# One decoder layer for a prompt and eight samples: the samples' attention in a written PE order, weights fetched by ScalarE, the first half's output projection and norm inside it

## Chip, cores and metric

The kernel runs on one core of a Trainium2 chip. The metric is the device time of one execution in microseconds, as the median of several runs. The engines are TensorE (PE in the profile, PEld for its weight loads), VectorE (DVE), ScalarE (ACT), GpSimd (POOL) and SyncE (SP, which here only issues DMAs).

## What is computed

One layer of a hybrid decoder on a prompt of 512 tokens and on 8 samples of 8 tokens with a cache of 4096 positions each: 576 token columns with the same weights. Cut to what matters here:

```python
h = x * (1 + ada[1]) + ada[0]
z = h @ w_in                       # latents, rotary key, short convolution, gates g_a and g_c
o = attention(...)                 # prompt: causal; samples: over 32 cached pages of 128 rows
y_a = o @ w_oa
y_c = (b_g * conv_y) @ w_oc
m = sigmoid(g_a) * y_a + sigmoid(g_c) * y_c
x = layer_norm(ALPHA * x + g1 * (m @ w_o), ln1_g, ln1_b)
h2 = x * (1 + sc2) + sh2
f = (silu(h2 @ w_ff1) * (h2 @ w_ff3)) @ w_ff2
y = layer_norm(ALPHA * x + g2 * f, ln2_g, ln2_b)
```

The samples' attention works in latent space, with an online softmax: for each page the scores of a sample's 64 query rows (8 heads x 8 tokens) against the page's 256 latent values and 32 rotary values per position, a running maximum and sum, and the weighted sum of the latents.

## The kernel before

Activations lie with features on the partitions and tokens in the columns. The 576 columns are two halves of 288 (`HT`): the first half is all prompt, the second is 224 columns of the prompt and the 64 of the samples. Every dense product is exact in fp32 from three matmuls (`mm3`, L117 to L119): the weight is split into a high and a low part (`wh` on ScalarE, L57; `wl` on VectorE, L60), the activations likewise. A weight comes in chunks of [128, 512] fp32, 256 KB, into a ring `wr` of three, and its split goes into rings `wh` and `wl` of three (`wload`, L99). A weight tile of 1024 columns and one half of the tokens take 24 matmuls of 288 columns.

The stages in order: conditioning and modulated input; latent projections; the prompt's attention (`prompt_units`, L496), among which the convolution's products and the rest of the conditioning are spread; the samples' attention (`sample_units`, L606), among which the gates' products, `w_oc` and the first half of `w_oa` are spread (`fill_gates`, `fill_oa`); then `w_o` and the first norm for the first half, `w_oa`, `w_o` and the norm for the second (loop at L916); then the feed forward and the second norm.

The samples' attention runs over 36 units: four pairs of samples, and for each pair one unit of the step's own 8 rows and eight units of 4 pages for each of the two samples. A page unit does, on PE: four score matmuls of 512 columns (L630, tile `sc`), where the two samples of the pair use different column halves of the array, two rotary score matmuls (L632), four transposes of the weights (L653), eight value matmuls (L661, tile `pv`), two samples again on two column halves. Between them VectorE takes the maximum (L646), ScalarE the exponential, and ScalarE copies the transposed weights to `pT`. A unit's pages are eight DMAs of 256 KB (L569) into a ring of seven tiles `raw`, and four gathers of rotary rows by GpSimd (L573) into a ring of three tiles `kr`.

What sets the order: a scheduler places each engine's instructions by what it expects to be ready, except on engines named in `tc.manual_schedule`, which keep the order of the code. In the samples' stage that is SP alone, so the pages' DMAs and the weights' DMAs stand in SP's queue as the code writes them, and PE's order is the scheduler's. `merge` (L745) spreads the filling units, each a whole product of 48 matmuls, over the attention's units.

In the prompt's attention two heads share the array's column halves in the value matmuls (L543); both heads' transposes (L536) and copies come before, head 0 first.

`Norm` (L812) adds the residual row by row. With `j0 == 8`, the first half's case, it subtracts the mean of all rows at once (`center`) and sums squares; else it takes the mean of the first rows off early.

## Time and profile before

| | |
|---|---|
| time, median of 3 runs (lowest, highest) | 1171.45 us (1170.65, 1172.48) |
| profiled execution, first to last instruction (span) | 1174.0 us |
| mean granted PE clock in it | 0.974 |
| PE busy | 1091.8 us, 93% |
| VectorE / ScalarE / GpSimd busy | 46% / 37% / 19% |
| moved by DMA | 190.07 MB, mean 162 GB/s |

The profile is of one execution; its times are those of the profiled execution, 2.55 us longer than the median. Records of matmuls overlap, since PE is pipelined, so a busy PE isn't a PE at its peak: how many matmuls end per microsecond says more. An fp32 matmul leaves two records; a matmul of split parts one. "Idle before" is the time for which an engine had nothing to run ahead of an instruction, with what ended it; in the chain of waits each row is a start, a length and what ran or was waited for.

### The profile page before, as it was taken

The numbers are of one execution on the slowest core, as the hardware profiler recorded it, in microseconds if no ns is written. First come the engines' busy times: TensorE is split into PE (matmuls) and PEld (weight loads), VectorE is DVE, ScalarE is ACT, GpSimd is POOL, SyncE is SP. The second block draws the span as 40 slices with busy tenths as digits, with TensorE's granted clock in tenths as the row PEclk, the third lists the DMA queues.
The fourth block names the chain that finished last, engine by engine and source line by source line (L and its number), as shares of the span: only waits on it lengthen the run. The fifth ranks groups of instructions, "written<-read, shape, count | busy, mean of one in ns | idle before, by whom it ended". The sixth has DMA issues, their size and how long they took to land.

```text
span 1174.0 us, 19868 instructions
## 1 busy us (share of the span) xinstructions
PE 1091.8 (93%) x7646; PEld 931.6 (79%) x7646; DVE 537.7 (46%) x1059; ACT 431.7 (37%) x859; POOL 225.1 (19%) x232
## 2 busy tenths in 40 slices
PE   6889999998798899989999889899999999999994
PEld 5878787785466466556569889899999999999994
DVE  3476354443132333332247787933233333355656
ACT  2474343435232522332346355332223222334433
POOL 1120000023442342441301421800000000001303
PEclk9999999999799998999999899999999999999998
DMA  9626354418389586696675423032222222455551
GB/s 366 209 96 204 122 185 141 140 46 311 106 294 321 170 300 214 220 310 244 203 239 172 159 73 108 3 107 91 90 72 79 100 75 72 118 178 150 157 181 54
DMA packets 84941, 190.07 MB, mean 162 GB/s; under 512 B 11600, under 2 KB 15568, under 8 KB 84848
## 3 DMA queue, kind: packets, MB, share of 16 engines
q1 hardware_dynamic: 80752, 180.42, 45.8%
q0 software_dynamic: 4096, 8.40, 2.3%
q8 instruction: 60, 0.98, 0.3%
q14 instruction: 33, 0.27, 0.1%
HBM read 185.72 MB, written 3.06 MB: 161 GB/s over the span
## 4 chain that ended last, share of the span: by engine, by line
PE 48%; DVE 7%; DMA 5%; issue 2%; ACT 1%; SPq 1%; POOL 0%; POOLq 0%; ACTq 0%; DVEq 0%
PE acc L117 10%; PE acc L118 9%; PE acc L119 9%; PE sc L117 4%; PE sc L119 4%; PE sc L118 4%; PE sc L630 3%; DMA wr<-in_w_ff_dram 3%; PE pv L661 3%; DVE xr L60 2%; DVE wl L60 2%; ACT wh L57 1%; PE sc L632 1%; SPq L569 1%; DMA raw<-in_page_dram 1%
## 5 line engine op out<-in xcount | busy, mean ns | idle before, releaser
L117 PE MATMUL acc<-h,wl 128*128 128x288 f32 x960 | 288.7, 302 | 14.1 <-DVE wl L60 8.5
L118 PE MATMUL acc<-h,wh 128*128 128x288 f32 x960 | 286.9, 299 | 2.0 <-DVE h L60 1.5
L119 PE MATMUL acc<-h,wh 128*128 128x288 f32 x960 | 284.7, 297 | 1.9 <-issue 1.9
L60 DVE TENSOR_TENSOR wl<-wr,wh 128x512 fp32r<-128x512 f32 (+1 forms) x186 | 178.7, 966 | 212.1 <-ACT wh L57 206.1
L57 ACT ACTIVATE wh<-wr 128x512 fp32r<-128x512 f32 (+2 forms) x196 | 156.6, 807 | 194.5 <-DMA wr<-in_w_ff_dram 58.7
L117 PEld LDWEIGHTS acc<-h,wl 128*128 128x128 f32 x960 | 181.5, 189 | 25.9 <-DVE wl L60 11.2
L118 PEld LDWEIGHTS acc<-h,wh 128*128 128x128 f32 x960 | 182.2, 190 | 7.3 <-issue 5.0
L119 PEld LDWEIGHTS acc<-h,wh 128*128 128x128 f32 x960 | 182.6, 190 | 3.1 <-issue 2.9
L573 POOL DMA_INDIRECT kr<-in_krT_dram,idx x128 | 122.7, 959 | 227.4 <-ACT krh L57 103.0
L117 PE MATMUL sc<-h,wl 128*128 128x288 f32 x336 | 99.9, 297 | 0.0
L118 PE MATMUL sc<-h,wh 128*128 128x288 f32 x336 | 99.4, 296 | 0.0
L119 PE MATMUL sc<-h,wh 128*128 128x288 f32 x336 | 99.1, 295 | 0.0
L630 PE MATMUL sc<-raw,qa 128*64 128x512 f32 x256 | 85.3, 634 | 3.2 <-DMA raw<-in_page_dram 1.8
L60 POOL TENSOR_TENSOR xr<-xr,h 128x288 f32<-128x288 f32 x16 | 17.2, 1098 | 366.1 <-ACT h L57 362.5
L117 PE MATMUL acc<-f,wl 128*128 128x288 f32 x288 | 85.9, 298 | 1.6 <-DVE wl L60 1.6
L118 PE MATMUL acc<-f,wh 128*128 128x288 f32 x288 | 84.9, 295 | 0.0
L119 PE MATMUL acc<-f,wh 128*128 128x288 f32 x288 | 84.7, 294 | 0.0
L661 PE MATMUL pv<-raw,pT 128*64 128x256 f32 x512 | 68.8, 401 | 12.5 <-ACT pT L57 6.3
L661 PEld LDWEIGHTS pv<-raw,pT 128*64 128x64 f32 x512 | 38.5, 143 | 37.7 <-issue 16.0
L119 PEld LDWEIGHTS sc<-h,wh 128*128 128x128 f32 x336 | 63.6, 189 | 0.0
L118 PEld LDWEIGHTS sc<-h,wh 128*128 128x128 f32 x336 | 63.3, 189 | 0.1
L117 PEld LDWEIGHTS sc<-h,wl 128*128 128x128 f32 x336 | 63.2, 188 | 0.1
(326 smaller groups left out, 1767.1 us busy)
## 6 DMA issues: line engine op xcount, KB each, us to landing
raw<-in_page_dram SPq DMA_DIRECT2D x256, 256.0 KB
wr<-in_w_ff_dram SPq DMA_DIRECT2D x76, 512.0 KB
wa<-in_w_ada_dram SPq DMA_DIRECT2D x40, 512.0 KB
wr<-in_w_in_dram SPq DMA_DIRECT2D x64, 256.0 KB
wr<-in_w_ff_dram SPq DMA_DIRECT2D x16, 384.0 KB
wr<-in_w_o_dram SPq DMA_DIRECT2D x18, 256.0 KB
wr<-in_w_oa_dram SPq DMA_DIRECT2D x16, 256.0 KB
x<-in_xT_dram SPq DMA_DIRECT2D x4, 576.0 KB
```

The costliest lines, as they stand in the source:

```text
L57: nc.scalar.activation(out=out, in_=in_, func=func, **kw)
L60: return (eng or v).tensor_tensor(out=out, in0=in0, in1=in1, op=op)
L117: mm(ps, lhsT=wl, rhs=xh, start=start, stop=False)
L118: mm(ps, lhsT=wh, rhs=xl, start=False, stop=False)
L119: mm(ps, lhsT=wh, rhs=xh, start=False, stop=stop)
L569: dma(out=raw[:, j], in_=a["page"][bass.ds(vs[GP * e + j], 1)].rearrange("a p d -> p (a d)"))
L573: g.indirect_dma_start(kr[:, 128 * j:128 * j + 128], None, a["krT"], bass.IndirectOffsetOnAxis(ap=idx[:, i:i + 1], axis=0))
L630: mm(ps[rows(e), :n], lhsT=qa[:, c, 2 * pa + e], rhs=rhs, start=c == 0, stop=False)
L632: mm(ps[:, :n], lhsT=qr[:, i, pa].rearrange("p e q -> p (e q)"), rhs=kx, start=False, stop=i == 0)
L661: mm(pv[rows(e), :KVL], lhsT=pT[:np_, j, e], rhs=rhs, start=j == 0, stop=j == nj - 1)
```

## The change

Four things are changed together.

1. In the samples' stage PE joins SP in the written order. `sample_units` becomes `sample_stage`: a unit is cut into `rotary` (the rotary rows' split, one unit earlier), `turn` (transposes and copy), `scores` (now with maximum, exponential and the running sum) and `values`. Between them the code calls `fill`: always behind the values, and in about half of the units also between `turn` and the next unit's `scores`.
2. The filling work is cut finer, into 59 pieces: half a gate tile (24 matmuls), one tile of `w_oc`, `w_oa` (12 matmuls) or `w_o`. Its weights are fetched by DMAs on ScalarE's queue.
3. `fill_wo` is new filling work: the first half's `w_o` products, residual, norm and modulated input, with its rows in the gates' tiles. So the loop over both halves behind the stage is now the second half alone. `w_o` is loaded in both places, where before its split was kept for both halves. The first half's rows and norm are copied by DMA to `xr` and `rst1` afterwards.
4. In the prompt's attention head 1's transposes come first.

```diff
-    def wload(src, n=1024, hl=None, tag="", to=None, eng=None):
+    def wload(src, n=1024, hl=None, tag="", to=None, eng=None, q=None):
...
-            dma(out=raw[:, :m], in_=src[:, c:c + m])
+            (q or dma)(out=raw[:, :m], in_=src[:, c:c + m])
...
+    wq = nc.scalar.dma_start
+
+    def dense_chunks(i, dst):
+
+        w = wload(a["w_in"][i - 3], q=wq)
+        pss = [ps_acc(), ps_acc()]
+        for p in range(2):
+            gpart(pss, w[p], hs, 0, range(4 * p, 4 * p + 4), 8)
+            if p:
+                for ps, sl in zip(pss, sls):
+                    act(dst[:, sl], ps[:, :HT])
+            yield 1
...
-                pts = []
-                for o in range(2):
+                pts = {}
+                for o in (1, 0):
...
+        S = scores(*units[0], pages[0], krn)
         for i, u in enumerate(units):
             if len(pages) <= i + AHEAD < len(units):
                 pages.append(load(*units[i + AHEAD]))
...
+            more = i + 1 < len(units)
+            if more:
+                kx = krn if units[i + 1][1] < 0 else rotary(pages[i + 1])
+            pT = turn(*u, S)
+            fill(2 * i)
+            if more:
+                S = scores(*units[i + 1], pages[i + 1], kx)
+            values(*u, pT, pages[i])
+            fill(2 * i + 1)
+            if u[1] < 0 and u[0] or not more:
+                attended(u[0] - 1 if more else u[0])
...
+    def fill_wo():
+
+        xa = gates["gc"][:, :, :HT]
+        wq(out=xa, in_=a["xT"][:, :, :HT])
+        for k in range(0, 8, 2):
+            g.tensor_scalar(out=xa[:, k:k + 2], in0=xa[:, k:k + 2], scalar1=ALPHA, scalar2=None, op0=MULT)
+        ga = gates["ga"]
+        names = ["ssum", "mu", "qs", "rs", "rr", "sq0", "sq1"]
+        p = Scratch(names, [ga[:, j, :HT] for j in range(8)])
+        n = Norm(p, xa, 0, 8)
...
+        for j in range(8):
+            w = wload(a["w_o"][j], q=wq)
+            ps = ps_acc()
+            gemm([ps], w, [halves(M[0])])
+            n.row(j, ps[:, :HT], ada[:, 2])
+            yield 1
+        n.center()
+        yield 1
+        yield 1
...
+        n.finish(rst, modulate(Q(), gs, bs, rst, H2, HT))
+        gates["xa"], gates["rst"] = xa, rst
+        yield 1
...
+    extra = 59 - 2 * PF - len(units)
+
+    def fill(s):
+
+        i = s // 2
+        if s % 2 or (i + 1) * extra // len(units) > i * extra // len(units):
+            next(F, None)
+    with tc.manual_schedule(engines={mybir.EngineType.SP, mybir.EngineType.PE}):
+        sample_stage(A3, qa, qr, pages, fill)
+        for _ in F:
+            pass
...
+    for j in range(8):
+        to_m(j, 1, woa(j, g), LN)
+    dma(out=xr[:, :, :HT], in_=gates["xa"])
+    dma(out=rst1[:, :HT], in_=gates["rst"])
...
+    def product(j):
+        w = wload(a["w_o"][j])
+        ps = ps_acc()
+        gemm([ps], w, [halves(M[1])])
+        return ps[:, :HT]
+    H2 = htile()
+    n = Norm(LN, xr[:, :, HT:], 1, 6)
+    n.rows(product, ada[:, 2])
+    n.sums()
```

What this does to the instructions is best seen in three places. First PE at the end of the prompt's attention, its last pair of heads; before, the rows are these (`sc<-ident,S` are transposes, `pv<-pt,vt` the value matmuls of one head and key block):

```order
L543 MATMUL pv<-pt,vt 64x512
L536 MATMUL sc<-ident,S 128x128 x3
L543 MATMUL pv<-pt,vt 64x512
L536 MATMUL sc<-ident,S 128x128 x2
L543 MATMUL pv<-pt,vt 64x384
L536 MATMUL sc<-ident,S 128x128 x2
L543 MATMUL pv<-pt,vt 64x384
```

Now PE has there:

```order
L553 MATMUL pv<-pt,vt 64x512 x2
L546 MATMUL sc<-ident,S 128x128 x4
L553 MATMUL pv<-pt,vt 64x384 x2
L546 MATMUL sc<-ident,S 128x128 x2
L553 MATMUL pv<-pt,vt 64x256 x2
```

The two heads' matmuls of a key block, which transposes parted, are now neighbours; so they are in all 16 key blocks, and in none before.

Second, the samples' stage. On PE before, in the pages of the second pair (`sc<-raw,qa` are score matmuls against pages, `sc<-krx,qr` the rotary ones, `pv<-raw,pT` the values):

```order
L630 MATMUL sc<-raw,qa 64x512
L653 MATMUL sc<-ident,S 128x128 x2
L630 MATMUL sc<-raw,qa 64x512 x3
L632 MATMUL sc<-krx,qr 128x512 x2
L653 MATMUL sc<-ident,S 128x128 x2
L630 MATMUL sc<-raw,qa 64x512
L661 MATMUL pv<-raw,pT 64x256 x8
L630 MATMUL sc<-raw,qa 64x512 x3
```

PE now, in a unit without the second piece of filling work, at the place where `w_oa` ends and `w_o` begins:

```order
L118 MATMUL acc<-ol,wh 128x288
L119 MATMUL acc<-oh,wh 128x288
L670 MATMUL sc<-ident,S 128x128 x4
L644 MATMUL sc<-raw,qa 64x512 x4
L646 MATMUL sc<-krx,qr 128x512 x2
L683 MATMUL pv<-raw,pT 64x256 x8
L117 MATMUL acc<-h,wl 128x288
```

All 32 page units have this form, with 24 (for `w_oa` 12) weight matmuls behind the values; before, 17 of the 32 had one score matmul apart from the other three. Between the first score matmul of the stage and the last values stand 900 weight matmuls before and 1152 now. ScalarE's queue, which had no DMA in it, reads in a unit of the gates now:

```order
L107 DMA wr<-in_w_in_dram 128x512
L57 ACTIVATE krh<-kr 128x512
L57 ACTIVATE S,sm<-sc,sm 128x512
L57 ACTIVATE sm<-sm 128x1
L57 ACTIVATE gct<-acc 128x288 x2
L57 ACTIVATE wh<-wr 128x512
L57 ACTIVATE pT<-sc 128x512
L107 DMA wr<-in_w_in_dram 128x512
```

A weight's split (`wh<-wr`) stands between the unit's exponential (`S,sm`) and the copy of the transposed weights (`pT`), and the next fetch into the same ring behind it. On GpSimd the four steps that scale the first half's residual (L909) stand behind all 128 gathers.

Third, the end of the stage. PE has there, from the last unit's scores on (`sc<-ga,ones` are the norm's sums, first of the rows and then of the squares, `sc<-ident,acc` transposes the last pair's attended latents, `sc<-raw` starts their product with the value weights):

```order
L644 MATMUL sc<-raw,qa 64x512 x4
L646 MATMUL sc<-krx,qr 128x512 x2
L683 MATMUL pv<-raw,pT 64x256 x8
L822 MATMUL sc<-ga,ones 128x288
L670 MATMUL sc<-ident,S 128x128 x4
L683 MATMUL pv<-raw,pT 64x256 x8
L837 MATMUL sc<-ga,ones 128x288
L699 MATMUL sc<-ident,acc 128x128 x2
L117 MATMUL sc<-raw 128x128
```

ScalarE has there (`ga<-gct` squares rows for the norm, `qs_80` and `raw` take the attended latents, `h` is a modulated row, `oh` the attention's result for the samples):

```order
L57 ACTIVATE ga<-gct 128x288 x8
L57 ACTIVATE qs_80<-sc 128x2x8x8 x2
L154 ACTIVATE ga<-ga 128x288
L57 ACTIVATE raw<-qs_80 128x8x16 x2
L155 ACTIVATE ga<-ga 128x288
L57 ACTIVATE h<-hf_6963,ga 128x288
L57 ACTIVATE h<-hf_6967,ga 128x288
L57 ACTIVATE h<-hf_6971,ga 128x288
L57 ACTIVATE h<-hf_6975,ga 128x288
L57 ACTIVATE oh<-sc 64x4x64
L57 ACTIVATE h<-hf_6979,ga 128x288
L57 ACTIVATE oh<-sc 64x4x64
```

The moved norm's last steps stand among the last steps of the attention; before, the norm's steps all came behind the stage, and the last transposes stood among `w_oa`'s matmuls of the first half.

More of the change, by code (lines that the diff above doesn't have):

```diff
@@ L687, in sample_units @@
         smt, acct = {}, {}
-        nxt = scores(*units[0], pages[0])
+        S = scores(*units[0], pages[0], krn)
         for i, u in enumerate(units):
@@ L745, in merge @@
-    def merge(s, f, nf, ns):
-        done, i = 0, 0
-        while i < ns and next(s, None) is not None:
-            i += 1
-            while done * ns < i * nf:
-                u = next(f, None)
-                if u is None:
-                    break
-                done += u
-    S, F = prompt_units(), fill_ca()
-    merge(S, F, 12, 18)
-    for _ in F:
-        pass
-    close(E2)
-    close(E)
-    close(CV)
-    gates["pool"] = pool("gc", side="right")
-    gates["gc"] = gates["pool"].tile([128, 8, T], F32, name="gct")
@@ L765, in build @@
-    RP = pool("raw", side="right")
-    F = itertools.chain(fill_gates(), fill_oa())
-    units = [(pa, gg) for pa in range(4) for gg in range(-1, NG)]
-    with tc.manual_schedule(engines={mybir.EngineType.SP}):
-        for _ in range(PF):
-            next(F)
-        wk2 = ring_tile("raw", [128, 2, 1024], F32R)
-        wk = wload(a["w_ukT"], to=(wk2[:, 0], wk2[:, 1]))
-        pages = [load(*u) for u in units[:3]]
-        next(S)
-        qa, qr = prepare(wk)
-        merge(S, F, P3, 1)
-        close(A2b)
-        close(A2)
-        A3 = gates["a3"] = pool("a3")
-        merge(sample_units(A3, qa, qr, pages), F, 21 - PF - P3, 37)
-        for _ in F:
-            pass
@@ L783, in build @@
[L783 to L800 removed]
+    M = []
@@ new lines, in fill_ca, with merge @@
+    def fill_ca():
+        ad = fill_ada()
+        for _ in fill_conv():
+            for _ in range(3):
+                next(ad, None)
+            yield 1
+        for _ in ad:
+            pass
+    def merge(s, f, nf, ns):
+        done, i = 0, 0
+        while i < ns and next(s, None) is not None:
+            i += 1
+            while done * ns < i * nf:
+                u = next(f, None)
+                if u is None:
+                    break
+                done += u
+    S, F = prompt_units(), fill_ca()
@@ new lines, in build @@
+    merge(S, F, 12, 18)
+    for _ in F:
+        pass
+    close(E2)
+    close(E)
+    close(CV)
+    gates["pool"] = pool("gc", side="right")
+    gates["gc"] = gates["pool"].tile([128, 8, T], F32, name="gct")
+    RP = pool("raw", side="right")
+    F = itertools.chain(fill_gates(), fill_oa(), fill_wo())
+    units = [(pa, gg) for pa in range(4) for gg in range(-1, NG)]
+    with tc.manual_schedule(engines={mybir.EngineType.SP}):
+        for _ in range(2 * PF):
+            next(F)
+        wk2 = ring_tile("raw", [128, 2, 1024], F32R)
+        wk = wload(a["w_ukT"], to=(wk2[:, 0], wk2[:, 1]))
+        pages = [load(*u) for u in units[:3]]
+        next(S)
+        qa, qr = prepare(wk)
+        next(S)
+        close(A2b)
+        close(A2)
@@ new lines, in build @@
+    affine(gs, bs)
+    h2 = [halves(gates["h2"])]
+    M.append(htile())
+    for j in range(8):
+        to_m(j, 1, woa(j, g), LN)
+    dma(out=xr[:, :, :HT], in_=gates["xa"])
+    dma(out=rst1[:, :HT], in_=gates["rst"])
+    close(gates["pool"])
+    close(YP)
+    close(OT)
+    close(wp[0])
+    wp[:] = [W2, 4, 1024, 2]
+    L2 = pool("ln2", side="right")
+    FG = pool("g", side="right")
+    place = [FG.tile([128, T], F32R, name=f"g{i}") for i in range(NG2)]
+    def product(j):
+        w = wload(a["w_o"][j])
+        ps = ps_acc()
+        gemm([ps], w, [halves(M[1])])
+        return ps[:, :HT]
```

274 lines of the change are left out of this document (122 added, 152 removed).

## The prediction

> **What bounds the kernel now.** I read the busy times by stretch first, cut where the trace changes its kind of work. The columns are length, then busy time and records of PE, of its weight loads, of VectorE (DVE), ScalarE (ACT) and GpSimd (POOL), then the granted clock, the DMA share and GB/s.
>
> ```profile
> span 1174.0 us, 19868 instructions
> ...
> 100.00:200.00 100.00, 100.00 (x724) 78.00 (x723) 49.51 (x127) 37.70 (x94) 2.53 (x12) 1.00 0.43 146
> 200.00:277.00 77.00, 75.53 (x519) 59.22 (x520) 34.32 (x98) 33.06 (x87) 8.51 (x10) 1.00 0.41 135
> 277.00:307.00 30.00, 22.62 (x102) 12.95 (x100) 7.69 (x19) 9.32 (x23) 15.99 (x16) 0.77 0.56 196
> 307.00:627.70 320.70, 296.06 (x1833) 200.42 (x1832) 103.91 (x258) 111.76 (x242) 98.55 (x104) 0.97 0.71 242
> 627.70:692.00 64.30, 55.01 (x375) 53.44 (x375) 53.04 (x93) 26.48 (x54) 24.35 (x12) 0.92 0.46 152
> 692.00:747.50 55.50, 49.73 (x358) 47.76 (x356) 48.10 (x101) 24.94 (x47) 15.37 (x14) 1.00 0.22 77
> 747.50:1066.00 318.50, 318.50 (x2383) 318.50 (x2384) 124.60 (x167) 96.37 (x150) 15.76 (x11) 1.00 0.30 95
> ```
>
> PE is the busy engine everywhere, but busy isn't full. In the last stretch, the feed forward, 318.5 us hold 2383 matmuls of 288 columns: 0.134 us each, with no idle time. That is PE's real price of one, and nothing from there on is touched. In the samples' attention (277 to 627.7, 350.7 us) PE looks 91% busy (22.62 + 296.06), though a fifth of the time carries no work at its real price. The next view lets one work that out: the chain of waits, cut to two page units; x counts the records, two for each fp32 matmul.
>
> ```profile
> 584.88 1.00 PE sc L630 x2
> 585.88 0.59 PE sc L653 x4
> 586.47 1.86 PE sc L630 x6
> 588.33 0.67 PE sc L632 x2
> 589.00 1.88 PE pv L661 x16
> 590.88 1.78 PE sc L630 x8
> 592.66 0.66 PE sc L632 x2
> 593.32 0.44 PE sc L653 x4
> ```
>
> The second unit's four score matmuls (L630) stand together and take 1.78 us: the two batches use the two column halves at once. The first unit's are parted by the transposes (L653) and take 1.00 + 1.86 = 2.86. Being parted costs 1.0 us, and the order of before parts a single score matmul from its three fellows in 17 of 32 units: 17 us. A whole unit is 1.87 + 0.66 + 0.44 + 1.88 = 4.85 us (with a mid value for the scores); 32 of them are 155. The four units of the step's own rows are a third as large by columns and rows, some 1.6 us each (an estimate), so 6.4. The order puts 900 weight matmuls into this stage: 900 x 0.134 = 120. Sum 282 of 350.7: **69 us are lost**. Parting takes 17. The first 30 us take 14: 7.4 idle, and a mean clock of 0.77 is half speed for 13.8 us, 6.9 of them lost. The other 38 are waits inside the units.
>
> **The change, part by part.** *Prompt's weighted values.* The rows are PE's timeline in one head pair: start, length, records.
>
> ```profile
> 132.53 1.07 PE L543 MATMUL pv<-pt,vt 128*64 128x512 f32 x2
> 133.90 0.86 PE L543 MATMUL pv<-pt,vt 128*64 128x384 f32 x2
> 138.32 0.65 PE L543 MATMUL pv<-pt,vt 128*64 128x256 f32 x2
> 140.09 0.65 PE L543 MATMUL pv<-pt,vt 128*64 128x256 f32 x4
> 143.17 0.43 PE L543 MATMUL pv<-pt,vt 128*64 128x128 f32 x2
> ```
>
> At 140.09 two matmuls of different heads happen to be neighbours and take the time of the wider one alone, 0.65. Before, the two heads of a key block never stand together; now all 16 pairs do. A head pair saves at most 1.07 + 0.86 + 0.65 + 0.43 = 3.0, four save 12, less where neighbours overlap already. PE is full at 100 to 200 but has gaps at 200 to 277, and the last head pair waits for ScalarE's copies. I take half, **6 us** (bounds 0 and 12).
>
> *The stage itself.* Work after: 155 + 6.4 for the units, as above but with no parted scores. The order puts 1152 weight matmuls between the units: 1152 x 0.134 = 154. That is 252 more than before, w_o of the first half (192) and what used to run after the stage. Sum 315.8. To it come two unknowns. The beginning lost 14 us, much of it waiting for first pages and rotary rows, which the change leaves where they are; the fixed order gives PE a weight chunk to run meanwhile. I take 8 (bounds 0 and 14). Then the waits inside a unit. Their prices are in the groups of instructions of 307 to 633: count, busy us, mean ns, idle before.
>
> ```profile
> L646 DVE TENSOR_REDUCE sm<-sc 128x1 f32<-128x512 f32 x30 | 20.7, 691 | 62.3 <-PE sc L632 52.2 <-issue 9.1 <-PE sc L653 1.0
> L57 ACT ACTIVATE S<-sc,sm 128x512 f32<-128x512 f32 x30 | 20.3, 675 | 2.8 <-DVE sm L648 2.2 <-DVE sm L60 0.6
> L57 ACT ACTIVATE pT<-sc 128x512 f32<-128x512 f32 (+1 forms) x34 | 19.3, 568 | 84.6 <-PE sc L653 60.0 <-remote 11.4 <-PE sc L632 5.5
> L573 POOL DMA_INDIRECT kr<-in_krT_dram,idx x104 | 98.5, 948 | 175.0 <-ACT krh L57 103.0 <-issue 51.2 <-DVE sm L648 17.6
> ```
>
> From the last score matmul to the transposes lie the maximum 0.69, two small steps, the exponential 0.68 and hand-overs: some 2.4 us. In the fixed order 1.88 of values and 3.2 of weights (24 x 0.134) always stand between: 5.1, so 2.7 are spare. Behind the transposes the copy of 0.57 is covered by the next scores and rotary matmuls, 2.5. By this no unit need wait; before, the waits cost 1.05 us a unit (38/36). I take 0.5 x 36 = **18 us** (bounds 0 and 38), since ScalarE also has the weights' splits in its queue and the w_oa chunks are only half as long. ScalarE and VectorE have room for what moves in: they were busy for 112 and 104 of 320.7 us, and the first half's eight residual rows and sums are 16 VectorE steps of half a microsecond. GpSimd's scaling of the residual now stands behind all 128 gathers; the last come two units ahead of need at 4 x 0.95 us, so I cost it at nothing. If a product had to wait for it, that would be once, under 5 us. Stage: 315.8 + 8 + 18 = 342 against 350.7: **-9** (bounds -35 and +17).
>
> *Behind the stage.* Before, 64.3 us pass from the last values to 692, where the second half's w_o products begin; both halves' rest, with a long wait for w_o, lies there.
>
> ```profile
> 641.82 4.00 DVE wl L60 x2
> 645.84 4.45 DMA wr<-in_w_o_dram
> 650.36 1.77 issue
> 652.12 3.38 DVE wl L60
> ...
> 677.37 0.42 ACT mu L57
> 677.81 5.82 DVE xr L60 x8
> ...
> 690.73 0.45 DVE qs L60
> ```
>
> After, only this is left: the samples' latents (24 short matmuls, 2.4), w_oa of the second half (96 x 0.134 = 12.9) and the wait for its last tile (2.1, four VectorE and ScalarE steps like the 0.45 above). But the tail is now bare. PE's order has the norm's sum of squares ahead of the last transposes; that waits for the mean and eight subtractions (0.42 + 5.82) while PE has 2.9 us of own work: 3.8 lost. Then copy, split and subtract before the latents' matmuls: 2.8. Then the split of their result stands behind seven modulated rows in ScalarE's and VectorE's queues, at two steps of 0.45 each 6.5. With 1.5 for exponential and copy of the last unit, and 5 for a clock that drops at such gaps (0.92 here) and slower VectorE steps beside GpSimd, 20 us are lost. Sum 37.4 against 64.3: **-27** (bounds -38 and -15). The 55.5 us from 692 on are taken over whole. What changes in them: w_o was kept split for both halves, and is now loaded and split again for the second. The first load stands on SP's queue behind the copies of the first half's rows and of its norm, which wait for that norm, some 9 us behind the last values; the landing (4.45) and split are still over before w_oa is done, some 35 us behind them. Each later load has a product of 24 x 0.134 = 3.2 us to hide behind, two deep in its ring: I cost them at nothing. Without a second place in the ring a product would cost 4.45 - 3.2 = 1.2 more, 10 in all.
>
> [...]
>
> **Sum.** -6 - 9 - 27 = -42 on the profiled span: 1174.0 becomes 1132.0. The median of the runs shown, 1171.45, is 2.55 less than that span, so the forecast time is **1129.5**.
>
> **Rivals.** *Pages become the bound.* In the stage 88 MB have to come: the pages 67.1 less 4.2 fetched before, gathers 8.4, 60 weight chunks 15.7, the residual 1.2.
>
> ```profile
> raw<-in_page_dram SPq DMA_DIRECT2D x256, 256.0 KB
> ...
> q0 software_dynamic: 4096, 8.40, 2.3%
> ```
>
> At the 242 GB/s of 307 to 627.7 that takes 365 us, 23 more than forecast: 1152. Against it: the share was 0.71 there, so 340 GB/s lie at 1.0; 342 us need only 258. For it: w_oa and w_o chunks come at twice the rate late in the stage. Chance 0.08. [...]
>
> *The order does not do what it says*: scores stand together, but the waits stay at 38 and the start at 14. The stage is then 26 longer: 1155. For it: the waits were there with a free order too. Chance 0.12.
>
> *ScalarE's queue becomes the bound, and the kernel slower.* A weight's fetch now stands in ScalarE's queue, and its split there waits for the landing, with the exponential behind it and PE's fixed order behind that. The chain of waits shows one such wait:
>
> ```profile
> 544.23 4.30 DMA wr<-in_w_in_dram
> 548.55 0.64 ACT wh L57
> 549.21 0.70 DVE wl L60
> ```
>
> If a split has to sit out a landing of 4.30, the 2.7 spare leave 1.6 lost. Once in each of 36 units that is 58: 1187. It decides from 42/1.6 = 26 of the 60 chunks on. Against it: the queue shows a fetch about ten ScalarE instructions ahead of its split, most of a unit. Chance 0.11. [...]
>
> **How the numbers follow.** The forecast, with the terms near their values, 1110 to 1148: 0.61. Waits and start gone and all of the prompt's pairs paid, 1129.5 - 18 - 8 - 6 = 1098: 0.08. The three rivals 0.08, 0.12, 0.11. The range leaves out the lower half of the best case and the slower rival, 0.15 in all: 1104 to 1162. The bounds of all terms at once would reach from 1086 to 1173, but nothing ties them to one another. A run tells 0.2% (2.3 us) from no change; the slower rival is almost wholly on that side, and 0.03 near its point of balance is counted as same: faster 0.87, same 0.03, slower 0.10.
>
> **What would show it.** Right: score matmuls of every page unit in 1.8 to 1.9 us; key blocks' pairs with equal starts; last values near 277 - 6 + 342 = 613; w_o of the second half from some 650; feed forward dense from about 705. Wrong: ScalarE idle long before a weight's split, PE idle before the transposes in most units, a DMA share of 0.9 and more with PE waiting for pages, or a gap of over 25 us between the last values and w_oa.

## The result, and the profile after

| | before | after |
|---|---|---|
| time, median (lowest, highest) | 1171.05 us (1169.56, 1172.48) | 1152.82 us (1150.73, 1158.98) |
| profiled execution: span | 1174.0 us | 1151.3 us (its time 1153.04) |
| mean granted PE clock in it | 0.974 | 0.971 |
| PE busy | 1091.8 us | 1064.1 us |
| moved by DMA | 190.07 MB | 195.07 MB |

The changed kernel takes 0.9852 of the time, 95% interval 0.9824 to 0.988: 18 us faster. The forecast was 1129.5, 42 us off the span; the direction was right and the time lies in the range, but less than half of the gain came. The busy times by stretch, cut where the trace of after changes its kind of work: the prompt's attention up to 275.80, the samples' stage from there to 631.20 (its first 28.7 us apart), what is left behind it to 728, and the feed forward. The columns are those of before.

```profile
span 1151.3 us, 19892 instructions
...
100.00:200.00 100.00, 100.00 (x755) 80.20 (x754) 50.42 (x130) 38.19 (x95) 1.70 (x12) 1.00 0.47 159
200.00:275.80 75.80, 66.57 (x474) 53.76 (x474) 34.26 (x93) 34.04 (x88) 8.30 (x10) 0.95 0.45 148
275.80:304.50 28.70, 20.98 (x109) 11.65 (x105) 7.10 (x17) 7.41 (x19) 16.04 (x16) 0.88 0.48 160
304.50:631.20 326.70, 311.16 (x2079) 222.49 (x2077) 136.32 (x321) 129.65 (x276) 109.27 (x111) 0.99 0.77 257
631.20:694.70 63.50, 47.59 (x302) 46.05 (x301) 47.92 (x96) 25.97 (x48) 15.13 (x9) 0.81 0.44 140
694.70:728.00 33.30, 29.16 (x191) 27.66 (x190) 27.14 (x44) 19.10 (x32) 18.18 (x14) 0.90 0.23 78
728.00:1044.00 316.00, 315.54 (x2385) 315.07 (x2384) 122.32 (x166) 97.58 (x151) 14.56 (x10) 1.00 0.30 96
```

Two things stand out. The prompt's last 75.8 us, full before (75.53 of 77.00), now have 9 us in which PE does nothing. And the stage is 28.70 + 326.70 = 355.4 us long where 342 were forecast; it was 350.7 before, with 252 weight matmuls fewer. Behind the stage the length is as forecast: the first `w_ff2` product begins at 987.1 us, 356 us behind the last values; before it was 1010.7 and 383.0, so 27 us less.

The chain of waits in two page units (start, length, what ran or was waited for):

```profile
439.99 1.87 PE sc L644 x8
441.86 0.66 PE sc L646 x2
442.52 1.88 PE pv L683 x16
444.40 0.33 PE acc L117
...
447.79 0.44 PE sc L670 x4
448.23 2.08 PE sc L644 x8
450.42 0.21 issue
450.64 0.62 ACT wh L57
451.26 0.49 ACT pT L57
451.80 1.95 PE pv L683 x16
```

The four score matmuls stand together in all 32 page units and take 1.87 us in 29 of them, as forecast (the 2.08 here is the chain's, which leaves PE before the rotary matmuls). But the second unit shows what the written order doesn't remove: the values wait for the copy `pT`, which stands behind a weight's split (`wh`) in ScalarE's queue, and the order gives PE nothing else. ScalarE and GpSimd in that unit:

```profile
448.41 0.94 POOL L583 DMA_INDIRECT kr<-in_krT_dram,idx  x1 [0.30 <-issue]
450.33 0.41 ACT L57 ACTIVATE ga<-acc 128x288 f32<-128x288 f32 x1 [3.69 <-PE sc L644]
```

ScalarE stands idle until 450.33, and then first copies a gate's product (`ga`). The matmuls of that product end by their records at 447.80 and the transposes at 448.23, but the trace has PE's signals for them at 450.31 and 450.38, behind a run of GpSimd's gathers. So the copy was late because the signals were late, and the split made it later. PE's waits in the whole stage (what waited, for what; us in total, times, longest):

```profile
PE sc L670 <- issue: 9.2, 3, 4.4
PE pv L683 <- ACT pT L57: 8.6, 11, 3.3
PE sc L670 <- ACT S L57: 3.0, 2, 1.8
```

The two rows on L670 are transposes that wait for the exponential (behind a wait written as "issue" no releaser was found). The timeline tells what three of the longest waits are. One is ahead of the stage, at the prompt's end:

```profile
265.50 0.63 ACT L57 ACTIVATE wh<-wr 128x512 fp32r<-128x512 f32 x1 [2.48 <-DMA wr<-in_w_in_dram]
269.18 0.34 ACTq L107 DMA_DIRECT2D wr<-in_w_in_dram  x1
269.56 1.47 ACT L57 ACTIVATE pt<-sc 128x512 f32<-128x512 f32 x3 [3.43 <-DMA raw<-in_page_dram]
270.21 0.90 PE L546 MATMUL sc<-ident,S 128*128 128x128 f32 x3 [6.04 <-ACT pt L57]
```

ScalarE's split waits for its weights, then the next fetch in its queue is issued only at 269.18, with the prompt's copies `pt` and PE behind it. The trace names what the fetch waited for: the wait ahead of it is for the semaphore that its own landing is to raise. A page's transfer, issued by SP, raised that semaphore last at 269.10, the wait ended at 269.12, and the copies' row puts its 3.43 us down to that page. So here a fetch held ScalarE's queue up until a page, fetched by SP, was in. ScalarE stops in the same way up to 556.45 (2.7 us) and, longest, behind the residual (9.0 us up to 583.53). There an earlier weight fetch of ScalarE's own had raised the semaphore last, at 556.38 and at 583.45:

```profile
567.91 0.62 ACTq L907 DMA_DIRECT2D gct<-in_xT_dram  x1
568.79 0.44 ACTq L107 DMA_DIRECT2D wr<-in_w_o_dram  x1
...
583.53 0.34 ACTq L107 DMA_DIRECT2D wr<-in_w_o_dram  x1
583.92 0.60 ACT L57 ACTIVATE pT<-sc 128x512 f32<-128x512 f32 x1 [9.40 <-DMA wr<-in_w_o_dram]
...
584.57 1.97 PE L683 MATMUL pv<-raw,pT 128*64 128x256 f32 x10 [3.30 <-ACT pT L57]
```

The third is the sigmoid over all gates, with the loads of ScalarE's tables around it; the unit's exponential stands behind it, and PE's transposes behind that:

```profile
529.94 4.05 ACT L57 ACTIVATE ga<-ga 128x4608 f32<-128x4608 f32 x1
...
535.04 1.28 ACT L57 ACT_TABLE_LOAD   x1
...
536.33 0.69 ACT L57 ACTIVATE S<-sc,sm 128x512 f32<-128x512 f32 x1
...
537.17 1.07 PE L670 MATMUL sc<-ident,S 128*128 128x128 f32 x4 [3.96 <-issue]
```

### The profile page after: what moved, and what is told of

It reads as the page before. It is cut to its first block, busy times and chain, and to the rows that moved or that the text cites. A ratio compares the mean times of both kernels' runs of the same rounds, so it can differ in the third digit from the quotient of the medians.

```text
span 1151.3 us, 19892 instructions
## 1 busy us (share of the span) xinstructions
PE 1064.1 (92%) x7646; PEld 917.1 (80%) x7646; DVE 542.9 (47%) x1068; ACT 442.8 (38%) x869; POOL 226.9 (20%) x236
## 2 busy tenths in 40 slices
DMA packets 88493, 195.07 MB, mean 169 GB/s; under 512 B 11696, under 2 KB 18864, under 8 KB 88400
## 4 chain that ended last, share of the span: by engine, by line
PE 72%; DVE 9%; DMA 8%; ACT 6%; issue 3%; SPq 1%; POOL 0%; ACTq 0%; POOLq 0%; DVEq 0%
PE acc L117 14%; PE acc L118 13%; PE acc L119 13%; PE sc L117 5%; PE sc L118 5%; PE sc L644 5%; PE sc L119 5%; PE pv L683 5%; DMA wr<-in_w_ff_dram 4%; DMA wr<-in_w_o_dram 2%; ACT wh L57 2%; DVE wl L60 2%; PE acc L198 2%; DVE xr L60 2%; PE sc L646 1%
## 5 line engine op out<-in xcount | busy, mean ns | idle before, releaser
L60 DVE TENSOR_TENSOR wl<-wr,wh 128x512 fp32r<-128x512 f32 (+2 forms) x192 | 182.0, 949 | 281.1 <-ACT wh L57 215.9
L119 PE MATMUL acc<-h,wh 128*128 128x288 f32 x960 | 283.9, 296 | 1.5 <-issue 1.5
L57 ACT ACTIVATE wh<-wr 128x512 fp32r<-128x512 f32 (+2 forms) x202 | 164.9, 819 | 243.4 <-PE acc L119 91.7
L119 PEld LDWEIGHTS acc<-h,wh 128*128 128x128 f32 x960 | 181.0, 189 | 3.5 <-issue 3.2
L119 PE MATMUL sc<-h,wh 128*128 128x288 f32 x336 | 99.3, 296 | 0.0
L119 PE MATMUL acc<-f,wh 128*128 128x288 f32 x288 | 84.8, 294 | 0.0
L683 PE MATMUL pv<-raw,pT 128*64 128x256 f32 x512 | 63.6, 391 | 8.6 <-ACT pT L57 8.6
L644 PE MATMUL sc<-raw,qa 128*64 128x512 f32 x256 | 67.3, 637 | 0.7 <-issue 0.7
L119 PEld LDWEIGHTS sc<-h,wh 128*128 128x128 f32 x336 | 63.4, 189 | 0.0
L683 PEld LDWEIGHTS pv<-raw,pT 128*64 128x64 f32 x512 | 34.4, 138 | 34.2 <-ACT pT L57 12.8
```

What stands on the lines that cost most here:

```text
L57: nc.scalar.activation(out=out, in_=in_, func=func, **kw)
L60: return (eng or v).tensor_tensor(out=out, in0=in0, in1=in1, op=op)
L119: mm(ps, lhsT=wh, rhs=xh, start=False, stop=stop)
L644: mm(ps[rows(e), :n], lhsT=qa[:, c, 2 * pa + e], rhs=rhs, start=c == 0, stop=False)
L683: mm(pv[rows(e), :KVL], lhsT=pT[:np_, j, e], rhs=rhs, start=j == 0, stop=j == nj - 1)
```

## The experiments

The times depend on the chip. Where the result was measured, and on chips A and C below, the kernel before takes 1168 to 1172 us; on B 1143 to 1144. So only ratios to the kernel before on the same chip, or times from one chip, are compared.

| run | what it is | chip | us | kernel before | ratio, 95% interval |
|---|---|---|---|---|---|
| e1_prompt | before, prompt's pairs alone | A | 1165.4 | 1170.0 | 0.9954 (0.9925 to 0.9983) |
| e2_sp | after, weights and residual on SP | A | 1201.6 | 1170.0 | 1.0277 (1.0225 to 1.0329) |
| e3_free | after, PE's order free | A | 1135.0 | 1170.0 | 0.9703 (0.9648 to 0.9757) |
| e4_res | after, residual on SP | A | 1153.6 | 1170.0 | 0.9844 (0.9799 to 0.9889) |
| e5_start | after, 4 pieces ahead of the stage | B | 1126.1 | 1143.5 | 0.9867 (0.9843 to 0.989) |
| e6_sig | after, sigmoid tile by tile | B | 1150.1 | 1143.5 | 1.0058 (1.004 to 1.0075) |
| e7_free_sp | free, weights and residual on SP | B | 1150.3 | 1143.5 | 1.0054 (1.0036 to 1.0071) |
| e8_free_nowo | free, first half's w_o behind the stage | B | 1132.7 | 1143.5 | 0.9918 (0.9894 to 0.9942) |
| c_after | after | B | 1140.0 | 1143.9 | 0.9966 (0.9954 to 0.9979) |
| c_start | as e5_start | B | 1126.0 | 1143.9 | 0.9834 (0.9816 to 0.9852) |
| c_free | as e3_free | B | 1119.8 | 1143.9 | 0.9781 (0.976 to 0.9802) |
| e12_tail | 4 pieces ahead, 3 products held back | B | 1131.8 | 1143.9 | 0.9893 (0.9874 to 0.9912) |
| d_before | before | C | 1167.9 | 1169.5 | 0.9991 (0.9962 to 1.0019) |
| d_after | after | C | 1155.4 | 1169.5 | 0.988 (0.9852 to 0.9908) |
| d_coarse | 4 pieces ahead, second pieces behind the values | C | 1152.5 | 1169.5 | 0.9845 (0.9813 to 0.9876) |
| d_early | free, filling work used up early | C | 1136.4 | 1169.5 | 0.9712 (0.9689 to 0.9735) |
| f_start | as e5_start | C | 1150.6 | 1171.6 | 0.9839 (0.978 to 0.9897) |
| f_free | as e3_free | C | 1133.0 | 1171.6 | 0.9695 (0.9633 to 0.9757) |

**The prompt's pairs alone.** The edit is the change's own lines in the kernel before: `for o in (1, 0)` around the transposes.

> Kernel before, with only the prompt's part of the change (head 1's transposes first, so that the two heads' value matmuls stand together). Theory A (the pairs pay, as forecast, and something else ate it in the changed kernel): in the changed kernel PE reaches the queries' matmul with sel at 257.3 us, before at 264.5, so the pairs have saved some 7 us by then; here nothing takes it back: the first score matmul of the samples at about 270.5 instead of 277.05, the time 1164 to 1166. Theory B (this stretch hangs on ScalarE's copies and VectorE, pairs are worth nothing): first score matmul at 276, time 1169 to 1171.

Measured: 4.6 us between the medians, 5.4 by the ratio (2 to 9 by its interval); the first score matmul of the samples starts at 270.7 us instead of 276.8. Theory A. The pairs pay about what was forecast, and the changed kernel loses it again at ScalarE's queue (265 to 270 us above): in e2_sp below, where these fetches stand on SP's queue, the first score matmul starts at 271.8, in the changed kernel at 275.8.

**Weights on SP's queue.** Two runs, with PE's order written and free:

```diff
-    wq = nc.scalar.dma_start
+    wq = nc.sync.dma_start
```

> Changed kernel, with the filling work's weights and the first half's residual fetched on SP's queue again instead of ScalarE's. Theory A (a fetch in ScalarE's queue has to wait until an earlier transfer has landed, with copies and exponentials behind it; seen at 266.1 to 269.2, 553.8 to 556.5 and 574.5 to 583.5 us): ScalarE's three waits of 3.1, 2.7 and 9.0 go, with PE's 6.0, 1.2 and 3.3 and the half clock behind them, so 10 to 14 us less: 1139 to 1143. Theory B (SP's queue, in which pages wait for their place in the ring, brings the weights too late for an order that PE may not leave): PE waits for weights in many units, 1160 or more. Theory C (neither matters): 1153.

> Free order of PE, with the filling work's weights on SP's queue again. With the written order this cost 48 us, 45 of them in the stage, at a handful of weights that came late. Theory A (late weights stop a written order only; a free one runs other work): 1135 to 1142. Theory B (the weights are late whatever the order, and ScalarE's queue carries a large part of the gain): 1155 or more.

Both times theory B: with the written order some 50 us slower than the changed kernel (1.0277 against 0.9852), with the free one 30 us (1150.3 against 1119.8 on B). SP's issues, ScalarE's split and PE in e2_sp:

```profile
545.93 2.22 SPq L579 DMA_DIRECT2D raw<-in_page_dram  x4
548.25 1.32 SPq L107 DMA_DIRECT2D wr<-in_w_oa_dram  x3
...
557.42 1.65 ACT L57 ACTIVATE wh<-wr 128x512 fp32r<-128x512 f32 x3
...
558.81 0.61 PE L117 MATMUL acc<-oh,wl 128*128 128x288 f32 x1 [9.07 <-DVE wl L60]
```

The weights are fetched behind pages and split 9.2 us after their issue. In the whole stage PE waits for such splits 38.5 us, in 12 places:

```profile
PE acc L117 <- DVE wl L60: 38.5, 12, 9.1
```

Without ScalarE's queue nothing of the gain is left: both runs are slower than the kernel before (1.0277 and 1.0054), in spite of the stops that this queue has of its own. It isn't bandwidth: with PE's order written the stage takes 407.7 us at 224 GB/s and a DMA share of 0.67 with SP's queue, 355.4 us at 250 GB/s and 0.75 with ScalarE's, and f_free moves 268 GB/s at 0.80 in it. What ScalarE's queue buys is that a fetch doesn't stand behind pages.

**PE's order free.**

```diff
-    with tc.manual_schedule(engines={mybir.EngineType.SP, mybir.EngineType.PE}):
+    with tc.manual_schedule(engines={mybir.EngineType.SP}):
```

> Changed kernel, with PE's order in the samples' stage left free again (only SP's is written). Theory A (the written order is what gains: 17 us of parted score matmuls and some 20 us of waits inside the units): 1170 to 1190, with score matmuls parted from their fellows in many units. Theory B (the finer pieces and the moved products give the gain, the written order little): 1150 to 1158, scores mostly together.

> Free order of PE once more, beside the changed kernel. Theory A (a written order without work at the stage's beginning is what costs, so free order and the written one with four pieces ahead come out alike): 15 to 20 us below the changed kernel, within 8 us of the run with four pieces ahead. Theory B (the written order costs inside the stage too): 10 us or more below the run with four pieces ahead.

> Free order, as the partner of the run above on the same chip: 0.967 to 0.974 of the kernel before where that takes some 1170 us, 0.976 to 0.980 where it takes 1143.

Theory A of the first falls, and B doesn't go far enough: the free order is faster than the written one by some 20 us on each chip (1119.8 against 1140.0 on B, 1133.0 against 1155.4 on C; 0.9703 against 0.9844 with e4_res on A). Score matmuls stand together in all 36 units here too, since the code is cut into `turn`, `scores` and `values`; the order need not be written for that. What the free order does otherwise is seen in PE's program: 12 weight matmuls or more (1.6 us) stand between transposes and values in 33 of 36 units, and 13 to 26 behind the values in 27. The written order puts a whole piece (24, of `w_oa` 12) behind the values of all units but the last two, but only 18 of the 36 have one between transposes and values. The free order is the fastest version measured, and was run on all three chips.

**Four pieces ahead of the stage.** In the free order 102 weight matmuls had moved ahead of the stage. Here the written order gets 96 there, where PE's order is free anyway:

```diff
         next(S)
+        for _ in range(4):
+            next(F)
         close(A2b)
...
-    extra = 59 - 2 * PF - len(units)
+    extra = 55 - 2 * PF - len(units)
```

> Changed kernel, PE's order in the stage still written, but four more pieces (96 weight matmuls) are taken out of the stage and given out before it, where PE's order is free. In the run with the free order 102 weight matmuls had moved there. Theory A (the written order leaves PE bare at the end of the prompt's attention: 6.0 us idle at 264, 4.4 at 277, half clock behind both): the first gap is filled, the time 1141 to 1146, some 8 to 10 us of the 18 between written and free order. Theory B (the difference lies inside the stage): 1151 to 1155.

> Written order with four more pieces ahead of the stage, once more, now beside the changed kernel. Theory A (PE is bare at the prompt's end): 8 to 12 us below the changed kernel. Theory B (the difference seen was the chip's): within 3 us of it.

> Written order, four pieces ahead of the stage. Where the kernel before takes some 1170 us: theory A (bare PE at the stage's beginning is most of the written order's cost there too): 0.974 to 0.979 of the kernel before, within 8 us of the free order. Theory B (inside the stage a written order cannot give way when a signal comes late, so it keeps most of its cost): 0.981 to 0.986, 10 us or more above the free order. Where the kernel before takes 1143 us: 0.983 and 6 us above the free order, as measured.

On B it takes 14 us off the changed kernel (1126.0 against 1140.0), more than theory A had, so there theory A holds: two thirds of the written order's cost of 20 lie at the stage's beginning. On C it takes 4 to 5 off, and the free order is 18 faster still: theory B. The program is the same, so the two traces can be laid side by side. The same unit on C, then on B:

```profile
294.31 0.60 PE L670 MATMUL sc<-ident,S 128*128 128x128 f32 x4
294.82 0.95 POOL L583 DMA_INDIRECT kr<-in_krT_dram,idx  x1 [0.30 <-issue]
...
303.16 0.63 ACT L57 ACTIVATE wh<-wr 128x512 fp32r<-128x512 f32 x1 [11.16 <-remote]
303.69 0.58 ACT L57 ACTIVATE pT<-sc 128x512 f32<-128x512 f32 x1
...
304.32 1.98 PE L683 MATMUL pv<-raw,pT 128*64 128x256 f32 x8 [6.89 <-ACT pT L57]
```

```profile
296.19 0.66 PE L670 MATMUL sc<-ident,S 128*128 128x128 f32 x4 [1.65 <-ACT S L57]
296.22 0.62 ACT L57 ACTIVATE wh<-wr 128x512 fp32r<-128x512 f32 x1
...
296.88 0.60 ACT L57 ACTIVATE pT<-sc 128x512 f32<-128x512 f32 x1
...
299.31 1.95 PE L683 MATMUL pv<-raw,pT 128*64 128x256 f32 x16
```

On B the copy starts as soon as the transposes end. On C ScalarE's split, which waits for PE's signal that the last weights are used, stands until 303.16, though by its records PE was through with them at 294.47 and with the transposes at 294.91. In the trace four signals of PE, for groups that end at 294.47, 294.91, 296.77 and 297.44 by their records, all arrive between 303.13 and 303.33. While these matmuls end, GpSimd issues its gathers of rotary rows, on both chips; on C that run of gathers ends at 300.77.

Late copies go with these gathers. Call a copy `pT` late if it starts more than 0.5 us after both the transposes and ScalarE's last instruction have ended. The twelve traces taken where the kernel before takes some 1170 us have 124 late copies, 12 in the first profile of after, and the transposes of all 124 end while a run of gathers is under way (the copy above isn't one of them, as it stands behind a split that was late); behind transposes that end outside the gathers no copy is late. On B the transposes of 23 to 28 of the 36 copies end among gathers, and in its eight traces no copy is late. So in these twenty traces late copies go with the gathers, and whether there are any goes with the chip. No run moves the gathers or leaves them out, so that they cause it isn't shown.

PE's waits for `pT` in the stage, on C with the written order, on C with the free order, and on B with the written one:

```profile
PE pv L683 <- ACT pT L57: 13.3, 12, 6.9
```

```profile
PE pv L683 <- ACT pT L57: 2.3, 2, 2.0
```

```profile
PE pv L683 <- ACT pT L57: 1.0, 2, 0.7
```

So on C late signals stop the written order (13.3 us), which in half of its units has nothing between; the free one (2.3 us) has its 12 matmuls there.

**The residual on SP's queue.**

```diff
-        wq(out=xa, in_=a["xT"][:, :, :HT])
+        dma(out=xa, in_=a["xT"][:, :, :HT])
```

> Changed kernel, with only the first half's residual (1.18 MB) fetched on SP's queue; the weights stay on ScalarE's. Theory A (the residual's packets stand ahead of a w_o chunk in the same queue, and the next fetch waits for that chunk's landing, 9.0 us at 574.5 to 583.5): that wait shrinks to under 1 us, PE's 3.3 us before the values at 581 and the half clock behind it go: last values 4 to 6 us earlier, time 1147 to 1149. Theory B (the residual delays the pages or the wait returns at another fetch): 1152 to 1155.

Theory B, no difference (0.9844 against 0.9852). The 3.3 us before the values shrink to 0.7, but a stop of ScalarE remains (6.7 us, up to 584.1), and in the whole stage the clock is at half for 23.9 instead of 13.7 us, worth 5 (an estimate: half of the 10.2 more).

**The sigmoid tile by tile.** The gates' sigmoid is worked out as 1 / (1 + exp(-x)):

```diff
-                    act(dst[:, sl], ps[:, :HT])
+                    act(dst[:, sl], ps[:, :HT], AF.Exp, scale=-1.0)
+                v.tensor_scalar(out=dst, in0=dst, scalar1=1.0, scalar2=None, op0=ADD)
+                v.reciprocal(out=dst, in_=dst)
...
-        act(gc, gc, AF.Sigmoid)
...
-        act(ga, ga, AF.Sigmoid)
```

> Changed kernel with the written order; the gates' sigmoids are worked out tile by tile as 1 / (1 + exp(-x)), the exponential in ScalarE's copy out of PSUM and the rest on VectorE, so the two sigmoids over 4608 columns (4.05 us each) and their loads of ScalarE's tables (1.28 each) go. Theory A (behind these two PE stands at the transposes, 1.8 us at 376 and 4.0 at 533, since its order may not go on): both waits and the half clock behind the second go, 6 to 8 us: 1145 to 1147. Theory B (the units' exponentials then wait for VectorE, which has 2 x 16 passes over 576 columns more): 1152 or more.

Theory B: 10 us slower than the changed kernel on B (1150.1 against 1140.0). VectorE and what stands behind it:

```profile
467.19 3.75 DVE L453 RECIPROCAL ga<-ga 128x576 f32<-128x576 f32 x1
470.85 0.63 DVE L654 TENSOR_REDUCE sm<-sc 128x1 f32<-128x512 f32 x1
...
474.71 1.11 PE L670 MATMUL sc<-ident,S 128*128 128x128 f32 x4 [2.42 <-ACT S L57]
```

The reciprocal of 576 columns takes 3.75 us, eight times the addition before it (0.46). Of the sixteen, eleven stand one or two steps ahead of a unit's maximum.

**The first half's products and norm behind the stage again**, with the free order:

```diff
-    F = itertools.chain(fill_gates(), fill_oa(), fill_wo())
+    F = itertools.chain(fill_gates(), fill_oa())
...
-    extra = 59 - 2 * PF - len(units)
+    extra = 48 - 2 * PF - len(units)
...
-        for _ in F:
+        for _ in fill_wo():
             pass
```

> Free order of PE, with the first half's w_o products and norm behind the stage again (still with pieces cut fine and weights on ScalarE's queue, 48 pieces instead of 59). Theory A (moving the products fills waits of the stage and shortens what is left behind it, as forecast: 27 us less behind): this gives much of it back, 1148 to 1160. Theory B (the waits would be filled by the finer pieces alone, and the moved products only change places): 1133 to 1140.

The times expected follow the 1135.0 of e3_free on A; on B the free order takes 1119.8, against 1132.7 here. So moving them is worth 13 us, as much as theory A has at its lower end and well above theory B.

**Behind the last values.** Two tries to fill what lies bare there. In e12_tail three pieces are held back, and the norm's sums stand where PE's order is free:

```diff
-            fill(2 * i + 1)
+            if more:
+                fill(2 * i + 1)
+            else:
+                next(F)
...
         latent(ol2, 3, 4)
+        next(F)
...
             split(src[rows(e), e], oTh[rows(e), :, SEQ:], oTl[rows(e), :, SEQ:])
+        next(F)
```

(with the four pieces ahead and `extra` from 50). In d_early PE's order is free, four pieces stand ahead and `extra` stays at 59, so the work is used up four places early and the norm ends before the last values.

> Written order, four pieces ahead of the stage, and the last three w_o products of the first half held back: one behind the last values, one behind the last transposes, one behind the latents' matmuls; the norm's sums then stand where PE's order is free, among w_oa's products. In the changed kernel PE is idle behind the last values for 4.6, 1.1, 2.4 and 7.7 us and its clock is half for 24 us, some 28 us lost. Theory A (the tail is bare because the written order has used up the filling work): 10 to 18 us below the run with four pieces ahead. Theory B (the waits only move, to the second half's products or the feed forward's start, since the first half's norm ends later): within 4 us of it.

> Free order of PE, four pieces ahead of the stage, and the filling work used up four places before the stage's end, so that the first half's norm is done before the last values. Theory A (behind the last values VectorE is the bound, as the norm's steps stand ahead of the latents' and the merged rows'): the four waits there (2.7, 1.1, 2.4 and 6.7 us with the free order) shrink to under 6 in sum, the last units lose 2 to 5 for want of filling work, the time 3 to 8 us below the free order alone (0.971 to 0.976 of the kernel before). Theory B (what is lost behind is the merged rows' own chain): within 3 us of the free order, 0.977 to 0.982.

Both times theory B is nearer. e12_tail is 6 us slower than the run with four pieces ahead (1131.8 against 1126.0). VectorE's steps and PE in it:

```profile
607.63 6.01 DVE L60 TENSOR_TENSOR gct<-gct,ga 128x288 f32<-128x288 f32 x8 [0.21 <-ACT ga L57]
...
619.25 1.30 PE L842 MATMUL sc<-ga,ones 128*128 128x288 f32 x2 [7.54 <-DVE ga L60]
...
626.83 0.58 PE L117 MATMUL acc<-oh,wl 128*128 128x288 f32 x1 [6.28 <-DVE mf L60]
```

The norm's subtractions and sums now stand among the merged rows' steps, and PE waits for VectorE at both. d_early is within 0.2% of the free order (0.9712 against 0.9695): in the profiles what stands behind the last values is 3.7 us shorter, and the stage 6.6 us longer, as the last units have no filling work.

**Fewer changes between kinds of matmul.** Four pieces ahead, and:

```diff
-            fill(2 * i)
             if more:
...
+            fill(2 * i)
             fill(2 * i + 1)
```

> Written order with four pieces ahead of the stage; the second piece of filling work of a unit, in 15 of the 36, stands with the first behind the values instead of between transposes and scores. Theory A (each place where PE changes between weight matmuls and the unit's own costs some 0.15 us, so 15 groups fewer are 30 changes, 4.5 us): 3 to 5 us below the run with four pieces ahead. Theory B (the second piece covers the copy behind the transposes or ScalarE's queue, and without it PE waits at the values or at the transposes): 3 us or more above it.

1152.5 against 1150.6 (f_start, same chip): neither theory at its size, no gain. c_after shows why theory A had nothing to save: on B, units without a second piece are 8.24 us apart by the starts of their values (8 times), units with one 11.43. A second piece so adds 3.19, which is no more than its 24 matmuls. But the forecast's prices give 4.85 + 24 x 0.134 = 8.07 for the first kind, so a unit's own price was 0.17 too low, 6 us in 36. The chain of waits in the first profile of after shows where most of it lies: the first weight matmul behind the values takes 0.33 us at 444.40, the others 0.13.

**Controls.** c_after, d_after and d_before are the two kernels themselves.

> The changed kernel itself, beside the next three on one chip: the kernel before took 1170 us on the chip of the first four runs and 1143 on that of the second four, so what these differ by has to be read beside the changed kernel on the same chip. Theory A (a chip is slower or faster for both kernels alike): 0.983 to 0.988 of the kernel before. Theory B (the chips differ in what the kernel before waits for, so the gain does too): nearer to 1 where the kernel before is fast, down to 0.98 where it is slow.

> The changed kernel once more, as the control of this group: 0.995 to 0.998 of the kernel before on a chip where that takes 1143 us, 0.982 to 0.988 where it takes 1170.

> The kernel before, with a profile of its own beside the changed kernel's on the same chip. On the chip where it takes 1143 us: theory A (the chips differ in the samples' stage alone, by signals from PE that ScalarE and VectorE see late there): stage about 325 to 332 us instead of 350.7, the rest within 3 us of the profile before. Theory B (they differ everywhere): the stretches of the prompt and the feed forward are 1 to 2% shorter too.

Theory B of c_after: where the kernel before is fast, the change gives 4 us, and 14 to 18 where it is slow. The changed kernel's stage is 339.6 us on B and 355.4 in the first profile. By the starts of the values, 22 of the 35 distances between neighbouring units are equal within 0.01 us; 6.3 us of the difference lie in the first unit, 3.8 at the sigmoid, the rest in steps of 0.3 to 1.2 in eleven others, nearly all without a second piece. Ahead of the stage and behind the last values the trace of B is 1.8 and 2.1 us longer. d_before came to chip C and shows only that its time repeats; the kernel before has no profile on B, so where it gains 26 us there stays open.

## Why the prediction was wrong, by its steps

| | forecast | measured (spans) |
|---|---|---|
| prompt, to the stage's first score matmul (276.8, now 275.8) | -6 | -1.0 |
| stage | -9 (to 342) | +4.5 (350.9 to 355.4) |
| behind it, to the first `w_ff2` product | -27 | -27.1 |
| from there to the end | 0 | +0.9 |
| span | -42 | -22.7 |
| from the span to the median | -2.55 | +1.5 |

- **Prompt's pairs, -6: right for the pairs, wrong for the kernel.** Alone they give 5.4. The step that failed is that nothing was counted against them: the fetches of the filling work, new in ScalarE's queue, put a stop of 3.1 us ahead of the copies `pt`, and PE stood idle for 6.0. The rival on ScalarE's queue had the engine and the mechanism (a weight with the exponential or a copy behind it) but not the cause. It named splits that sit out a landing, in up to 36 units; what happened was three fetches that waited for another transfer's landing (3.1, 2.7 and 9.0 us).
- **The stage, 342: the failing step, with 13 of the 23 us missed.** It measured 355.4: the waits and the price of a unit were too low. "By this no unit need wait", with 18 for the waits and 8 for the beginning, has 26: in the first profile of after PE stands idle 9.2 + 8.6 + 3.0 and 2.4 in smaller rows, 23 us, and 13.7 us at half clock cost 7 more, 30 in all. The 4.85 of a unit left out 0.17, 6 in all. The sum 315.8 + 30 + 6 = 352 leaves 3 unexplained. Behind the waits stands a wrong reading of the trace of before. Its 38 us of waits inside the units were put down to the order; some 24 of them are idle time, 8 are lost at half clock and 6 are the same 0.17 a unit. And part of the idle time came from late signals, which a new order doesn't remove: four copies `pT` started 3.7 to 4.7 us after the transposes and ScalarE were done, and behind three of them PE stands idle for 3.1, 2.4 and 1.3 us. On B the same program has a stage of 339.6 us, with 12.7 idle and 4 lost at half clock. That is near the 342 by luck: the waits were 10 too high for that chip, the units 6 too low.
- **The written order was taken for the source of the gain.** e3_free, c_free and f_free show that it costs some 20 us; the finer cut keeps the scores together without it, ScalarE's queue is worth 30 us with the free order (e7_free_sp) and the moved products 13 (e8_free_nowo). The rival "the order doesn't do what it says", 1155 with a chance of 0.12, came nearest in time. Its stage (368) was too long, and it had no loss in the prompt.
- **Behind the stage, -27: right in sum, partly by luck.** The tail is bare, as forecast, and its waits mostly hang on VectorE; filling it with matmuls made it worse. But the waits put at 3.8, 2.8 and 6.5 measured 4.6, 1.1 and 2.4. A wait of 7.7 us for the weights of `w_oa`, whose split stands behind merged rows in ScalarE's queue, wasn't foreseen, and half clock cost some 8 where 5 were taken for it and slower VectorE steps. These were seen too: in the first profile of after `mf<-mf,gct` (128x288) takes 0.46 us with GpSimd idle (672.6) and 0.91 to 1.11 beside GpSimd's splits and scalings (652.7 to 661.4). From the last values to the second half's `w_o` it is 39.6 us where 37.4 were forecast, and from there to `w_ff2` 2.4 less than before.
- **No bound from pages:** DMA share 0.77 in the stage, and no long wait of PE for a page. The 0.08 was fair.
- **From span to time:** the median of before was taken 2.55 below its profiled span, but an execution's time is 1.7 above its span (1153.04 and 1151.3 here). So the execution profiled before must have been some 4.7 us above its median. Of the 23 us by which the forecast missed, 4 come from this, 5 from the prompt, 13 from the stage and 1 from the end.
- **The clock.** In the stage, behind the wait of 3.96 that ends at 537.17, the granted clock is half from 537.3 to 540.7, 3.4 us. Behind the stage the waits of 4.6 (to 635.8) and 7.7 (657.6 to 665.3) have half clock from 636.2 to 649.9 and from 660.1 to 670.4, 13.7 and 10.2 us, in which the weight matmuls of `w_oa` end 0.24 us apart (647.4 to 649.4) instead of 0.133 (650.5 to 653). The 5 us of the prediction for the clock and VectorE's steps were too mild.

## What to carry to other kernels

Before an order is written out by hand for an engine, run the finer pieces with the order left free: here the pieces, their queue and the moved products gave the gain, and the written order took 20 us of it back. On one chip most of that was at the seam into the stage, where PE stood bare; on another most was inside the stage, where half of the units had nothing to run while a copy was late. Where an order must be written, cover that seam first; some filling work in both waits of every unit, as the free order has it, is the next thing to try (no run here wrote such an order). And take a forecast's waits apart by what ends them before a new order is credited with removing them.

## What the runs showed of the hardware

- The same program took 1140.0 us on one chip and 1155.4 on another, with equal durations of single instructions: in the first profile of after and in c_after the mean of a weight's split on ScalarE is 627 ns in both, of VectorE's maximum 690 and 691, of a weight matmul (L119) 294 in both. Where it is slower, PE's signals in the samples' stage reach ScalarE up to 8.7 us after the matmuls end by their records (f_start, 294.47 to 303.13), four of them within 0.2 us. Of the 36 copies `pT` in the first profile of after, 12 started more than 0.5 us after both the transposes and ScalarE's last instruction had ended; on B none did. All 12, and all 124 in the twelve traces of such chips, belong to transposes that ended during a run of GpSimd's gathers (0.95 us each, 0.3 apart). Why the gathers go with late signals on some chips and not on B is open.
- In the first profile of after three fetches issued from ScalarE waited for the semaphore that their own landing raises, until an earlier transfer had raised it, with all that stood behind them in ScalarE's queue: 3.1 us (up to 269.18) for a page that SP had issued, 2.7 and 9.0 (up to 556.45 and 583.53) for an earlier fetch of ScalarE's own.
- In e6_sig VectorE's reciprocal of 128x576 takes 3.75 us, 6.5 ns a column; the addition of a scalar over the same columns 0.46.
